# The gate projection of an SSD mixer, with tokens instead of channels on the partitions

## The chip, the cores and the metric

The kernel runs on one core of a Trainium2 chip. The metric is the time of one execution on the device, in microseconds (us). The kernel before was timed in three runs: 1871.24 us median, from 1871.17 to 1872.91.

## The reference

A two-layer diffusion backbone over 256 latent tokens and 256 context tokens, 1024 wide. Layer 0 mixes tokens with a gated DeltaNet, layer 1 with a Mamba-2 state space mixer (SSD); each layer ends in a mixture of 16 experts. The change lies in the second mixer, of which only the latent output is needed, since it is the last layer:

```python
def ssd_mixer(hx, hc, w_in, conv_w, conv_b, a_log, dt_bias, d_skip, norm_g, w_out):
    ...
    def project(h):
        p = h @ w_in
        z = p[..., :SSD_INNER]
        xbc = jax.nn.silu(depthwise_conv(p[..., SSD_INNER:SSD_INNER + SSD_CONV_CH], conv_w) + conv_b)
        ...
    def mix(h, h0f, h0b):
        z, xs, bm, cm, dt = project(h)
        yf, hf = ssd_scan(xs, dt[:, :, 0], A[0], bm, cm, h0f)
        yb, hb = ssd_scan(_rev(xs), _rev(dt[:, :, 1]), A[1], _rev(bm), _rev(cm), h0b)
        y = yf + _rev(yb) + d_skip.astype(F32).reshape(SSD_GROUPS, r)[..., None] * xs.astype(F32)
        y = y.reshape(b, t, SSD_INNER).astype(h.dtype) * jax.nn.silu(z)
        return rms_norm(y, norm_g) @ w_out, hf, hb
```

`z` is the gate: 2048 channels, projected from the 1024 inputs. `y`, the scan's result, is multiplied by silu(z), scaled by the root mean square over all 2048 channels of a token, and goes through the output projection `w_out`. Everything is in float32.

## The kernel before

A float32 matmul is made of three matmuls of split operands: a tile is copied to the type fp32r (the high half, `H`), and the remainder is the low half (`L`); the products H·H, L·H and H·L are added up. `split` (L512 on) makes the halves of a weight tile: ACT copies (L520), POOL subtracts (L522), or DVE for items whose number is in the table `DV`. The inputs lie ready in halves as `hT`, with channels on the partitions, in eight tiles of 128 channels and 512 tokens (256 of them latent).

The second mixer is a pipeline of items (`pipeline`, L534). Each item is one block of output channels of the input projection: its weights come from the queue of SP into a tile `wst` of 1 MB (two items share one), are split one item ahead, and `proj` issues 24 matmuls. Its later steps (`post`) follow, one each, behind the splits of the following items, and between items `tick` moves the waiting generators on. After the items for B and C come 16 x items (512 tokens each, `xitem`) and 16 z items (256 tokens each, `zitem`), in the order of the table `SSD_ORDER`: two of x and two of z by turns, z four pairs behind, so that the last eight z items come alone. When two x items are done, `ssd_group` is spawned: the scan for one head group of four heads in six steps. In them, `ga` (DVE) and `gw` (ACT, DVE, POOL) are weighted inputs and decay matrices, `hm` in `gb` is the state between the chunks (two POOL products, L1837, then a DVE sum, L1838), `yi` and `ya` are PE's products between and within chunks, POOL adds twice (L1855), DVE adds `ya` (L1862), PE transposes the sum, and ACT copies it to `y` (L1868) with channels on the partitions.

A z item's first step takes silu of the projection (ACT) and multiplies `y` by it (DVE, L1742). The second takes the square (ACT) and adds it to `sqs` on POOL (L1748), and makes the halves yH (ACT, L1751) and yL (DVE, L1752), scaled by the norm's gain, which is a value per partition there. The sums over channels are matmuls with ones, in `ssd_out`. At z item 13 the first tile of `w_out` is split (`ssd_wsplit`, wH on ACT, wL on DVE, L1881) and `ahead` spawned, which makes the expert layer's gate block (`moe_block`, gb, L1252) and the rows of the residual gate (`gate_rows`, g1). Then `ssd_out` runs the output projection into `acc`; after it comes the routing, and the expert layer, whose weights are loaded ahead (`moe_stream(1, 19)`) into the pool of 21 tiles of 1 MB, as they become free.

Each engine works its queue in the order in which the code issues; an instruction that waits holds up all that stand behind it on its engine.

## Time and profile before

| | us |
|---|---|
| median of three runs | 1871.24 |
| the profiled execution | 1866.32 |
| its span, first to last instruction | 1864.4 |
| PE busy in the span | 1579.6 |
| DVE busy | 833.0 |
| ACT busy | 453.7 |
| POOL busy | 405.6 |

The profiled execution lies 4.9 us below the median; sums made from its rows are set against its own time. PE's share of 85% is a mean over stages with different limits: in the expert layers the weights' loading sets the pace, in the mixers work on PE and its neighbours does. The second mixer's x and z items run from about 1176 to 1340 us, the output projection from there to 1391 us.

### The profile page before, as it was taken

How to read it: one execution, taken by the hardware profiler on the slowest of the kernel's cores; microseconds unless marked ns; L12 is line 12 of the kernel's file. 1: busy time of each engine (PE TensorE's matmuls, PEld its weight loads, DVE VectorE, ACT ScalarE, POOL GpSimd, SP SyncE). 2: the span in 40 equal slices, each digit the busy share in tenths (PEclk: the TensorE clock that was granted, in tenths of full speed). 3: DMA queues.
4: the chain of work that ended last, by engine and by line, in shares of the span. 5: the costliest groups of instructions: out<-in, count | busy, mean ns of one | idle time of the engine just before them, and what ended most of it. 6: DMA issues, size and time to landing. Idle time of an engine off the chain costs nothing.

```text
span 1864.4 us, 28211 instructions
## 1 busy us (share of the span) xinstructions
PE 1579.6 (85%) x11666; PEld 969.7 (52%) x11666; DVE 833.0 (45%) x1678; ACT 453.7 (24%) x825; POOL 405.6 (22%) x378
## 2 busy tenths in 40 slices
PE   7999888996899999989887999999899766666665
PEld 5666567864645443322226877878776332222222
DVE  4446987778632232212127877777753120111113
ACT  4552233223211100000005554666521000000001
POOL 3242255755000000000003444566400000000001
PEclk9999898998998999999998999999999887677788
DMA  9947522101888999999996441122698999999996
GB/s 305 377 161 273 181 68 91 48 1 69 310 326 355 378 383 420 419 420 420 419 409 211 158 136 46 46 69 91 236 372 351 418 419 419 419 419 420 419 419 257
DMA packets 136597, 520.18 MB, mean 279 GB/s; under 512 B 12237, under 2 KB 72022, under 8 KB 88598
## 3 DMA queue, kind: packets, MB, share of 16 engines
q1 hardware_dynamic: 136070, 517.58, 71.3%
q8 instruction: 92, 1.51, 0.3%
q0 software_dynamic: 400, 0.81, 0.1%
q14 instruction: 35, 0.29, 0.0%
HBM read 515.21 MB, written 3.15 MB: 278 GB/s over the span
## 4 chain that ended last, share of the span: by engine, by line
PE 40%; DMA 33%; DVE 16%; issue 5%; ACT 3%; POOL 2%; SPq 1%; POOLq 0%; ACTq 0%; DVEq 0%
PE ps L153 19%; DMA ew<-in_moe_w_down_dram 11%; DMA ew<-in_moe_w_up_dram 11%; PE proj L153 10%; DMA ew<-in_moe_w_gate_dram 10%; PE acc L153 3%; PE ps L157 2%; DVE adacc L384 2%; DVE tmpa L792 2%; DVE tmpb L791 2%; DMA adaq<-in_ada_w_dram 1%; PE pp L153 1%; POOL wr L522 1%; PE vn L153 1%; PE qs L153 1%
## 5 line engine op out<-in xcount | busy, mean ns | idle before, releaser
L153 PE MATMUL ps<-ew,xs 128*32 128x256 f32 (+1 forms) x3072 | 408.5, 522 | 113.9 <-DMA ew<-in_moe_w_gate_dram 58.9
L153 PE MATMUL proj<-hH,wr 128*128 128x512 f32 (+2 forms) x1312 | 380.5, 369 | 6.6 <-POOL wr L522 4.6
L153 PEld LDWEIGHTS ps<-ew,xs 128*32 128x32 f32 (+1 forms) x3072 | 136.5, 132 | 365.7 <-issue 149.7
L153 PEld LDWEIGHTS proj<-hH,wr 128*128 128x128 f32 (+1 forms) x1312 | 236.7, 190 | 57.5 <-issue 8.7
L153 PE MATMUL ps<-ew,moeblk 128*32 128x256 f32 (+3 forms) x1824 | 201.9, 455 | 47.0 <-DMA ew<-in_moe_w_down_dram 44.9
L522 POOL TENSOR_TENSOR wr<-wst,wr 128x1024 fp32r<-128x1024 f32 x74 | 184.4, 2496 | 247.4 <-ACT wr L520 247.2
L153 PE MATMUL proj<-hL,wr 128*128 128x512 f32 (+2 forms) x656 | 237.5, 362 | 0.4 <-DVE hL L2104 0.4
L1504 DVE TENSOR_TENSOR hid<-ps,sg 128x512 f32<-128x512 f32 (+1 forms) x32 | 17.9, 558 | 463.0 <-issue 271.5
L1481 DVE SCALAR_TENSOR_TENSOR ys<-ps,moeblk 32x256 f32<-32x256 f32 (+2 forms) x114 | 69.2, 607 | 225.9 <-PE ps L153 224.7
L153 PEld LDWEIGHTS ps<-ew,moeblk 128*32 128x32 f32 (+1 forms) x1824 | 75.4, 129 | 167.9 <-issue 86.4
L153 PEld LDWEIGHTS proj<-hL,wr 128*128 128x128 f32 (+1 forms) x656 | 125.1, 191 | 19.5 <-issue 1.0
L1503 ACT ACTIVATE sg<-ps 128x512 f32<-128x512 f32 (+1 forms) x32 | 15.7, 491 | 464.3 <-PE ps L153 464.3
L518 POOL CAST wr<-wdt 128x512 fp32r<-128x512 f32 x1 | 0.9, 869 | 529.4 <-PE ps L153 529.4
L2126 POOL DMA_DIRECT2D fgr<-in_final_norm_g_dram x1 | 0.6, 590 | 459.1 <-DMA ew<-in_moe_w_down_dram 459.1
L520 ACT ACTIVATE wr<-wst 128x1024 fp32r<-128x1024 f32 x79 | 82.9, 1053 | 20.3 <-POOL wr L522 9.7
L981 POOL TENSOR_SCALAR S<-S,gdnblk 128x128 f32<-128x128 f32 x128 | 74.7, 605 | 36.5 <-DVE S L990 36.4
L153 PE MATMUL ps<-G,X 128*128 128x128 f32 (+1 forms) x480 | 65.1, 298 | 9.5 <-DVE G L1362 9.5
L170 ACT ACTIVATE moeblk<-ps 128x512 f32<-128x512 f32 (+1 forms) x16 | 7.8, 491 | 265.3 <-PE ps L157 265.3
L153 PEld LDWEIGHTS ps<-G,X 128*128 128x128 f32 x480 | 62.8, 210 | 11.1 <-DVE G L1362 9.6
L560 DVE SCALAR_TENSOR_TENSOR u<-proj,prm,u 128x510 f32<-128x510 f32 (+1 forms) x56 | 39.5, 705 | 43.7 <-ACT u L558 43.6
L1382 ACT ACTIVATE xs<-ps,adaT 128x128 f32<-128x128 f32 (+1 forms) x60 | 21.3, 435 | 132.2 <-PE ps L153 120.6
L558 ACT ACTIVATE u<-proj,prm 128x512 f32<-128x512 f32 (+1 forms) x56 | 36.4, 651 | 51.0 <-PE proj L153 51.0
(417 smaller groups left out, 2189.7 us busy)
## 6 DMA issues: line engine op xcount, KB each, us to landing
ew<-in_moe_w_gate_dram SPq DMA_DIRECT2D x128, 1024.0 KB, 19.9
ew<-in_moe_w_up_dram SPq DMA_DIRECT2D x128, 1024.0 KB, 19.9
ew<-in_moe_w_down_dram SPq DMA_DIRECT2D x118, 1024.0 KB, 19.9
adaw<-in_ada_w_dram SPq DMA_DIRECT2D x40, 1024.0 KB, 9.0
wst<-in_ssd_w_in_dram SPq DMA_DIRECT2D x24, 1024.0 KB, 5.4
wst<-in_gdn_w_in_dram SPq DMA_DIRECT2D x16, 1024.0 KB, 10.9
adaq<-in_ada_w_dram SPq DMA_DIRECT2D x8, 1024.0 KB, 11.8
ew<-in_moe_w_down_dram SPq DMA_DIRECT2D x32, 256.0 KB, 6.7
```

What stands on the lines that cost most here:

```text
L153: self.nc.tensor.matmul(out, lhsT, rhs, start=start, stop=stop)
L157: self.nc.tensor.transpose(out, in_, self.ident[:k, :k])
L384: nc.vector.scalar_tensor_tensor(a, w[:, kk], c, a, op0=OP.mult, op1=OP.add)
L520: self.nc.scalar.activation(wr[:, 0, :, :m], src, AF.Copy)
L522: (self.nc.vector if dve else self.nc.gpsimd).tensor_tensor(wr[:, 1, :, :m], src, wr[:, 0, :, :m].bitcast(FT), op=OP.subtract)
L558: nc.scalar.activation(u[:, :n], p[:, :n], AF.Copy, scale=taps[1])
L560: nc.vector.scalar_tensor_tensor(v(u, 1, T), v(p, 0, T - 1), taps[0], v(u, 1, T), op0=OP.mult, op1=OP.add)
L791: nc.vector.tensor_tensor(t, bc(Lp[:, rows, j], n), mid(X[:, j, cols], m), op=OP.mult)
L792: nc.vector.tensor_tensor(X[:, rows, cols], X[:, rows, cols], t, op=OP.subtract)
L981: nc.gpsimd.tensor_scalar(S[d][1][:, h, hg, :], S[d][0][:, h, hg, :], self.eGl[:, h, d, q:q + 1], None, op0=OP.mult)
L1382: nc.scalar.activation(o, a, AF.Identity, bias=B, scale=A)
L1481: nc.vector.scalar_tensor_tensor(cols(grp["ys"][s][o], c), blk(y[q, :FW]), tg[o, 1], blk(g2[q, :FW]), op0=OP.mult, op1=OP.mult)
```

## The change

The z projection is done the other way round. `hT` becomes the stationary operand, 128 tokens at a time, and 512 columns of weights move, so that the result has tokens on the partitions. There are four blocks of 512 channels, each in two items by half of the inputs (q = 0 to 7, b = q // 2, j = q % 2), with 24 matmuls of 512 columns each, which add up in two PSUM banks `zp` that are held from the first item of a block to the end of the second. A weight tile is [512 inputs, 512 channels], and the halves lie in two tiles `wzH` and `wzL` of 128x2048. In the table, one q item follows two x items; q4 to q7 come alone at the end.

`ssd_group` ends with the sum of yt and ya, written straight into `y`, which now has tokens on the partitions; its transposes and copy are gone. The gate is done once for each block: for each 128 tokens silu (ACT), product (DVE), square with an accumulated sum over the row (ACT). One step later (`turn`), `y` is transposed to channels in two PSUM banks, and yH and yL are made from these (ACT and DVE). The sums of squares need one DVE reduction instead of the POOL sums and the matmuls with ones. The low halves of q5, q6 and q7 are made by DVE, the others by POOL. The first split of `w_out` and `ahead` are issued in the gate step of q6.

```diff
     for p in range(8 + lag):
-        o += [(k, 2 * q + j) for k, q in ((1, p), (0, p - lag)) if 0 <= q < 8 for j in range(2)]
+        o += [(1, 2 * p + j) for j in range(2) if p < 8] + [(0, p - lag)] * (p >= lag)
...
-SOW = 10
+SOW = 5
...
-ZT = 2
+ZT = 4
...
-DV = (9,11,13,15)
+DV = (5, 6, 7)
...
     def wload(self, n):
...
+            if isinstance(c, tuple):
+                b, j = c
+                t = self.u([128, KD // 2, 512], "wst")
+                src = ws["w"][j * 512:(j + 1) * 512, b * 512:(b + 1) * 512]
...
     def split(self, it, dve=None, hi=None):
 
         src = it["src"]()
+        if "acc" in it:
+            wr = [self.u([128, KD // 2, 512], f"wz{n}", FR) for n in "HL"]
+            self.nc.scalar.activation(wr[0], src, AF.Copy)
+            (self.nc.vector if it["dve"] else self.nc.gpsimd).tensor_tensor(wr[1], src, wr[0].bitcast(FT), op=OP.subtract)
+            it["wr"] = wr
+            return
...
+    def proj_tok(self, it, hT):
+
+        acc, j, wr = it["acc"], it["j"], it["wr"]
+        if j == 0:
+            acc += [self.ps("zp") for _ in range(2)]
+        it["p"] = acc
+        for k in range(4):
+            for t in range(2):
+                for a, b in ((0, 0), (0, 1), (1, 0)):
+                    self.mm(acc[t], hT[b][4 * j + k][:, t * 128:(t + 1) * 128], wr[a][:, k, :],
+                            start=j + k + a + b == 0, stop=j == 1 and k == 3 and a == 1)
...
                 if ct == 0:
-                    st["y"] = [self.u([128, 8, 256], f"y{j}") for j in range(2)]
+                    st["y"] = [self.u([128, 2, 1024], f"y{j}") for j in range(2)]
...
-        def zitem(ct):
-            def act(it):
...
-                z = self.cu([128, 256], "z")
-                y = st["y"][ct // 8][:, ct % 8]
-                nc.scalar.activation(z, it["p"][:, :256], AF.Silu)
-                nc.vector.tensor_tensor(y, y, z, op=OP.mult)
-
-            def fin(it):
-                y = st["y"][ct // 8][:, ct % 8]
-                sq = st["sq"]
-                nc.scalar.activation(sq[:, 1], y, AF.Square)
-                nc.gpsimd.tensor_tensor(sq[:, 0], sq[:, 0], sq[:, 1], op=OP.add)
-                H, L = st["yH"][ct // 8][:, ct % 8], st["yL"][ct // 8][:, ct % 8]
-                g = self.sng[:, ct:ct + 1]
-                nc.scalar.activation(H, y, AF.Copy, scale=g)
-                nc.vector.scalar_tensor_tensor(L, y, g, H.bitcast(FT), op0=OP.mult, op1=OP.subtract)
...
+        def zitem(q):
+            b, j = divmod(q, 2)
+            h = b // 2
+
+            def gate(it):
...
+                if q == SOW:
+                    st["sow"] = [self.ssd_wout(n) for n in range(3)]
+                if q == 6:
+                    st["ws"] = [self.ssd_wsplit(st, 0)]
+                    self.spawn(ahead(), 1)
+                if j == 0:
+                    return
...
+                for t in range(2):
+                    z, y = self.cu([128, 512], "z"), st["y"][h][:, t, b % 2 * 512:b % 2 * 512 + 512]
+                    nc.scalar.activation(z, it["p"][t], AF.Silu)
+                    nc.vector.tensor_tensor(y, y, z, op=OP.mult)
+                    nc.scalar.activation(z, y, AF.Square, accum_out=st["sq"][:, t, b:b + 1])
+
+            def turn(it):
+                it["yp"] = [self.ps() for _ in range(2)]
+                for n in range(4):
+                    for t in range(2):
+                        c = b % 2 * 512 + n * 128
+                        self.tr(it["yp"][n // 2][:, n % 2 * 256 + t * 128:n % 2 * 256 + t * 128 + 128], st["y"][h][:, t, c:c + 128])
+                for n in range(4):
+                    ct = 4 * b + n
+                    y, g = it["yp"][n // 2][:, n % 2 * 256:n % 2 * 256 + 256], self.sng[:, ct:ct + 1]
+                    H, L = st["yH"][h][:, ct % 8], st["yL"][h][:, ct % 8]
+                    nc.scalar.activation(H, y, AF.Copy, scale=g)
+                    nc.vector.scalar_tensor_tensor(L, y, g, H.bitcast(FT), op0=OP.mult, op1=OP.subtract)
+            return dict(src=lambda: self.wtile((b, j)), acc=zacc[b], j=j, post=[gate] + [turn] * j, dve=q in DV,
+                        ticks=ZT if q >= 8 - LAG else XT * 2)
...
-        nc.vector.tensor_tensor(fl(yt), fl(yt), intra, op=OP.add)
-        yield
-        p = self.ps()
-        for j in range(2):
-            for c in range(2):
-                self.tr(p[:, j * 256 + c * 128:j * 256 + c * 128 + 128], yt[:, c, j * 128:(j + 1) * 128])
-        nc.scalar.activation(fl(st["y"][g // 4][:, g % 4 * 2:g % 4 * 2 + 2, :]), p, AF.Copy)
+        o = st["y"][g // 4][:, :, g % 4 * 256:g % 4 * 256 + 256]
+        nc.vector.tensor_tensor(o, yt, intra.rearrange("p (c n) -> p c n", c=2), op=OP.add)
...
-                p = self.ps()
-                for t in range(2):
-                    self.mm(p[:, t:t + 1], st["sq"][:, 0, t * 128:(t + 1) * 128], self.ones[:, 0:1])
-                self.rsqrt(r2[:, 0:2], p[:, 0:2], 1.0 / 2048, EPS)
+                nc.vector.tensor_reduce(r2[:, 0:2], st["sq"], axis=AX.X, op=OP.add)
+                self.rsqrt(r2[:, 0:2], r2[:, 0:2], 1.0 / 2048, EPS)
```

POOL's queue about the scan of the seventh head group, the second last, before:

```order
L522 TENSOR_TENSOR wr<-wst,wr 128x1024
L1748 TENSOR_TENSOR sqs<-sqs 128x256
L1806 TENSOR_TENSOR gw<-gw,Gs 128x512
L1837 TENSOR_TENSOR gb<-gb,ssdblk 128x256 x2
L1840 TENSOR_TENSOR gb<-xt,gw 128x256 x2
L522 TENSOR_TENSOR wr<-wst,wr 128x1024
L1855 TENSOR_TENSOR gb<-gb,ga 128x512 x2
```

The same place after:

```order
L1892 TENSOR_TENSOR gb<-gb,ga 128x512 x2
L535 TENSOR_TENSOR wr<-wst,wr 128x1024
L525 TENSOR_TENSOR wzL<-wst,wzH 128x2048 x2
L1843 TENSOR_TENSOR gw<-gw,Gs 128x512
L1874 TENSOR_TENSOR gb<-gb,ssdblk 128x256 x2
L1877 TENSOR_TENSOR gb<-xt,gw 128x256 x2
L1892 TENSOR_TENSOR gb<-gb,ga 128x512 x2
```

`wr` and `wzL` are low halves of weights, `sqs` the sums of squares. Between two groups' additions to gb (L1855, L1892) the sums and the small splits are gone, and two splits of 128x2048, for q3 and q4, stand together ahead of this group's gw and gb. The second of them is written into the tile in which q3's high half lay.

DVE's queue ahead of the copy of the ada rows to `gb` (L1252 before, L1279 after), before:

```order
L1742 TENSOR_TENSOR y_7468<-y_7468,z 128x256
L1752 SCALAR_TENSOR_TENSOR yL<-y_7468,prm_239,yH 128x256
L522 TENSOR_TENSOR wr<-wst,wr 128x1024
L1881 TENSOR_TENSOR wL<-sow,wH 128x2048
L1742 TENSOR_TENSOR y_7468<-y_7468,z 128x256
L1752 SCALAR_TENSOR_TENSOR yL<-y_7468,prm_239,yH 128x256
L1252 COPY gb<-adaT_151 128x256
```

After, with the copy in the seventh row:

```order
L525 TENSOR_TENSOR wzL<-wst,wzH 128x2048
L1772 TENSOR_TENSOR y_7468<-y_7468,z 128x512 x2
L1888 TENSOR_TENSOR ga<-yi,ssdblk 128x512 x2
L1900 TENSOR_TENSOR y_7468<-gb,ya 128x2x256
L1913 TENSOR_TENSOR wL<-sow,wH 128x2048
L1786 SCALAR_TENSOR_TENSOR yL<-ps,prm_239,yH 128x256 x4
L1279 COPY gb<-adaT_151 128x256
L172 COPY g_9128<-ps 128x512
L1772 TENSOR_TENSOR y_7468<-y_7468,z 128x512 x2
L1786 SCALAR_TENSOR_TENSOR yL<-ps,prm_239,yH 128x256 x4
```

Products and low halves of y came by turns, item by item; now two products and four low halves stand together, with a split for q7 ahead of the products of block 2, and the split of w_out (L1913) ahead of its four low halves.

ACT's queue at the end of the mixer, before, from the copies of `moe_block` and `gate_rows` on:

```order
L1258 ACTIVATE moeblk<-ps 128x256
L170 ACTIVATE g_9384<-ps 128x512
L1741 ACTIVATE z<-proj 128x256
L1747 ACTIVATE sqs<-y_7468 128x256
L1751 ACTIVATE yH<-y_7468,prm_239 128x256
L1741 ACTIVATE z<-proj 128x256
L1747 ACTIVATE sqs<-y_7468 128x256
```

After, from the first split of w_out on:

```order
L1912 ACTIVATE wH<-sow 128x2048
L1785 ACTIVATE yH<-ps,prm_239 128x256 x4
L1285 ACTIVATE moeblk<-ps 128x256
L170 ACTIVATE g_9128<-ps 128x512
L1771 ACTIVATE z<-zp 128x512
L1773 ACTIVATE z,sq<-y_7468 128x512
L1771 ACTIVATE z<-zp 128x512
L1773 ACTIVATE z,sq<-y_7468 128x512
L1785 ACTIVATE yH<-ps,prm_239 128x256 x4
L1912 ACTIVATE wH<-sow 128x2048 x7
```

The last block's silu, for all its 512 channels, stands behind the copy of g1 (L170), and squares and silus now stand by turns, with DVE's product between them.

## Rows read from the trace of the kernel before

**Rows 1.** Windows: length; busy PE, PEld, DVE, ACT, POOL (instructions); clock; DMA share; GB/s

```profile
1211.10:1243.90 32.80, 31.15 (x185) 26.28 (x183) 21.81 (x39) 20.09 (x35) 24.35 (x20) 1.00 0.21 65
1243.90:1269.76 25.86, 25.82 (x152) 22.31 (x152) 17.98 (x35) 15.62 (x29) 17.81 (x14) 1.00 0.27 82
1299.84:1320.00 20.16, 17.23 (x118) 15.18 (x118) 14.42 (x30) 11.88 (x24) 12.10 (x11) 1.00 0.54 194
1320.00:1340.25 20.25, 16.38 (x146) 15.80 (x144) 14.50 (x15) 10.32 (x19) 8.76 (x8) 0.92 0.39 124
1390.80:1409.00 18.20, 13.80 (x109) 10.95 (x113) 12.12 (x49) 2.78 (x9) 0.00 (x0) 0.81 0.73 293
1440.00:1840.00 400.00, 267.79 (x2744) 109.82 (x2745) 49.55 (x107) 11.94 (x32) 0.59 (x1) 0.78 1.01 417
```

**Rows 2.** Timeline of SP's queue around 1400 us: start, length, what it issued

```profile
1390.98 0.89 SPq L1225 DMA_DIRECT2D ew<-in_moe_w_down_dram  x2
1408.96 2.92 SPq L1228 DMA_DIRECT2D ew<-in_moe_w_gate_dram  x4
```

**Rows 3.** Timeline of PE at the mixer's end; in brackets idle time, releaser

```profile
1311.31 1.56 PE L153 MATMUL yi<-gb,CT 128*128 128x256 f32 x6 [0.85 <-DVE gb L1838]
...
1319.37 0.66 PE L157 MATMUL ps<-ident,gb 128*128 128x128 f32 x4 [1.85 <-DVE gb L1862]
...
1332.78 2.36 PE L153 MATMUL ps<-ident,gb 128*32 128x64 f32 x32 [3.17 <-DVE gb L1252]
```

**Rows 4.** The chain that ended last: start, length, engine, tile, line, instructions

```profile
1258.38 0.86 PE ps L153 x4
...
1262.11 1.73 PE yi L153 x8
1263.84 1.73 PE ya L153 x16
1265.57 0.45 PE ps L157 x4
1266.02 2.87 PE proj L153 x24
...
1269.76 5.48 PE proj L153 x24
```

**Rows 5.** Groups by line and shape, 1140 to 1400 us: busy us, mean ns; idle

```profile
L1855 POOL TENSOR_TENSOR gb<-gb,ga 128x512 f32<-128x512 f32 x16 | 20.9, 1308 | 20.4 <-DVE ga L1851 19.8
...
L1881 DVE TENSOR_TENSOR wL<-sow,wH 128x2048 fp32r<-128x2048 f32 x8 | 18.7, 2358 | 11.6 <-ACT wH L1880 11.6
...
L1748 POOL TENSOR_TENSOR sqs<-sqs 128x256 f32<-128x256 f32 x16 | 15.7, 978 | 14.7 <-ACT sqs L1747 14.7
...
L1880 ACT ACTIVATE wH<-sow 128x2048 fp32r<-128x2048 f32 x8 | 15.0, 1907 | 15.0 <-PE acc L153 15.0
...
L1752 DVE SCALAR_TENSOR_TENSOR yL<-y,prm,yH 128x256 fp32r<-128x256 f32 x16 | 13.4, 837 | 1.2 <-ACT yH L1751 1.2
...
L1806 POOL TENSOR_TENSOR gw<-gw,Gs 128x512 f32<-128x512 f32 x8 | 10.5, 1315 | 7.5 <-ACT gw L1804 7.5
...
L1837 POOL TENSOR_TENSOR gb<-gb,ssdblk 128x256 f32<-128x256 f32 x16 | 9.5, 615 | 0.0
...
L1751 ACT ACTIVATE yH<-y,prm 128x256 fp32r<-128x256 f32 x16 | 8.1, 508 | 0.0
...
L1838 DVE TENSOR_TENSOR gb<-gb,ps 128x512 f32<-128x512 f32 x8 | 5.5, 688 | 27.3 <-POOL gb L1837 27.3
```

**Rows 6.** The same view, POOL, the first 1000 us: a subtract of 128x2048

```profile
L1120 POOL TENSOR_TENSOR wL<-gwo,wH 128x2048 fp32r<-128x2048 f32 x4 | 18.0, 4520 | 9.4 <-ACT wH L1119 9.4
```

**Rows 7.** Timeline of DVE in the period of the second window

```profile
1260.39 0.69 DVE L1838 TENSOR_TENSOR gb<-gb,ps 128x512 f32<-128x512 f32 x1 [3.02 <-POOL gb L1837]
...
1268.12 2.00 DVE L1742 TENSOR_TENSOR y<-y,z 128x256 f32<-128x256 f32 x1
```

**Rows 8.** Timeline of POOL in the same period

```profile
1267.43 2.39 POOL L522 TENSOR_TENSOR wr<-wst,wr 128x1024 fp32r<-128x1024 f32 x1
```

36 lines of the change are left out of this document (17 added, 19 removed).

## The prediction

> **What bounds the kernel now.** I began with the windows view by stage [rows 1]. From 1440.00 to 1840.00 us the expert layer moves 417 GB/s at a DMA share of 1.01: that part waits for bytes alone. In the stretch before it, 1390.80 to 1409.00, the share is only 0.73, and the list of DMA issues says why [rows 2]: SP issues the last two expert loads at 1390.98 and the next four at 1408.96. The 21 one-megabyte tiles of the pool are full by then, and loading goes on when the first experts have been used. So the prefetch already waits for the mixer, and the end of the program moves one for one with the end of the second mixer. What ends the mixer is read from the same windows: in a period in the middle (1243.90 to 1269.76) PE is busy 25.82 of 25.86 us; in the last two stretches 17.23 of 20.16 and 16.38 of 20.25. In the middle PE's own work sets the pace; at the end it idles 2.93 + 3.87 = 6.80 us. The timeline of PE there names the releaser of the longest waits [rows 3]: a DVE result, gb of the scan twice and gb of the ada block, the last for 3.17 us. The tail is a chain through POOL, DVE and ACT with matmuls in its gaps.
>
> **The change part by part.**
>
> *Matmuls.* Sixteen items of 24 matmuls with 256 columns at 2.87 us become eight of 24 with 512 columns; an x item of that shape takes 5.48 [rows 4]: 16 x 2.87 - 8 x 5.48 = 45.9 - 43.8 = 2.1 us less. Transposes: 32 of the scan's result go, 32 of the gated y come, no difference. The Trainium skill (TensorE: Matmul & The Clock Gate, section "Wait — 56ns, not 53.3ns?") gives a fixed cost of about 2.5 ns a matmul on top of the columns. By it, 192 fewer matmuls would save an estimated 0.5 us instead of 2.1; the rows here show more, and I keep the rows.
>
> *Work taken off.* POOL loses 16 adds of 978 ns, 15.7 us [rows 5], and ACT eight copies; DVE's y products become half as many and twice as wide. In the middle none of these engines bounds anything (POOL 17.81 of 25.86), so I count nothing there. At the end the freed time is inside the waits below. The weight loads stay 1 MB each and are hidden at a DMA share of 0.21 to 0.54 [rows 1]; the longer runs per row cost nothing. The tensor_reduce for the ones-matmuls is a small operation off the path.
>
> *What the order does.* Two or more z items used to stand between the scan's steps; now only one q item of 5.48 us stands in a period, and q4 to q7 close the mixer with one scan step or so between. I followed PE through the changed program, engine queues beside it, with the durations of the rows. The waits that end on PE:
>
> (a) POOL before q4. The low half of q4's weights (128x2048) lies in the slot of q3's high half, so POOL's subtract cannot start before q3's matmuls end. Behind it in POOL's queue stand gw and gb of the seventh head group, which DVE's hm add and PE's second yi matmuls need. A 128x2048 subtract on POOL took 4.52 us [rows 6], gw 1.32, two gb 1.23, the DVE add 0.69 [rows 5]: 7.8 us after q3, covered by 1.3 us of matmuls (0.86 of ps and a quarter of yi's 1.73 [rows 4]). Before, the same add waited 3.02 us for POOL [rows 7], but a z item of 2.87 us covered it. **6.4 us.** Low bound 3, if the wide subtract runs at DVE's 2.36 us; high bound 8, if DVE holds it up.
>
> (b) After that, y's product for block 1 stands on DVE behind the y sum (as 0.69), which waits for one more yi result on DVE (0.69) and two POOL adds (2 x 1.31), and behind q5's low half (2.36); then product, square, second Silu and second product in turn (0.5 to 0.7 each, by DVE's 128x512 add at 0.69 and ACT's H step, 0.51 at half that width). From q3's end y is ready at 7.8 + 1.3 + 0.7 + 2.6 + 0.7 + 2.4 + 2.5 = 18.0; PE is at its transposes at 7.8 + 1.3 + 1.73 + 0.45 + 5.48 = 16.8, after the rest of yi, ya, the transposes of u, and q4 [rows 4]: **1.2 us** (0 to 3).
>
> (c) The turn to channels makes ACT's H and DVE's L alternate, since two pairs share a PSUM bank: 4 x (0.51 + 0.84) = 5.4 us at the means of before [rows 5], and all of it ahead of the copy that feeds ga of the last group (four DVE products, later two more). One q item covers the first part: **3.1 us** over both ga steps (1 to 4).
>
> (d) The products of block 2 wait on DVE behind q7's low half (2.36), of which a yi and ya step covers little, as PE comes to the transposes right after them: **1.9 us** (0 to 3).
>
> (e) The ada block's gb copy stands on DVE behind the first w_out split (2.36) and four L steps. Before, it stood behind one split and two L steps and PE waited 3.17 us [rows 3]; now **4.9 us** (3 to 6).
>
> (f) The last block's Silu stands on ACT behind g1's copy, whose matmuls PE does after q7. Then copy, Silu, product, square, Silu, product in series, 0.5 to 0.7 each as in (b): **4.0 us** (2 to 5) with nothing but 0.9 us of transposes for PE. Before, the last item needed only its own two halves, and PE was in w_out at once.
>
> (g) The second w_out split (1.91 on ACT, 2.36 on DVE) waits for the last turn: **1.8 us** (0 to 3).
>
> (h) In the step of x12, ACT's square waits for DVE's product, which shares time with POOL's wide split; the Silu of x11 and then the copy for ga come late: **3.8 us** (0 to 6). Rows of before show what such a meeting is like: POOL's subtract from 1267.43 for 2.39 us, DVE's product from 1268.12 for 2.00 [rows 7, 8], so both end within 0.3 us of each other, whereas DVE's 128x512 add, twice as wide, takes 0.69 on average. The Trainium skill (SBUF — State Buffer, section "Who interferes with whom") calls the port pair an exclusive lock, which the first takes for its whole instruction. This trace agrees.
>
> (i) In the periods of q1 and q2 the hm add is reached with no z item ahead of yi: **2.4 us** for both (0 to 3).
>
> Sum of the waits 6.4 + 1.2 + 3.1 + 1.9 + 4.9 + 4.0 + 1.8 + 3.8 + 2.4 = 29.5 us. They take the place of PE's idle time of before: 6.80 at the end and 32.80 - 31.15 = 1.65 in the period at 1211.10 [rows 1], 8.5 in all. With the matmuls: 29.5 - 8.5 - 2.1 = **+18.9 us**. All low bounds together give 3 + 0 + 1 + 0 + 3 + 2 + 0 + 0 + 0 = 9, hence 9 - 8.5 - 2.1 = -1.6; all high ones 41 - 10.6 = +30.
>
> The profiled run of before took 1866.32 us with a span of 1864.4, the median of the three runs is 1871.24. The sum against the profiled run is 1885.2; the same 18.9 us on the median give 1890.1, the forecast.
>
> **The rivals.**
>
> *PE bound and waits hidden* (chance 0.17). The matmuls' 2.1 us remain as a gain, and half the idle time of the end goes because POOL and ACT have less to do: 1871.2 - 2.1 - 3.4 = 1865.7. For it: PE has no idle time in the middle period, and POOL loses 15.7 us. Against it: the subtract of q4 has no other place in its queue, and cover is gone where PE already waits.
>
> *Only the slot and the end count* (0.20): (a), (e) and (f) alone, 6.4 + 4.9 + 4.0 - 6.8 - 2.1 = +6.4, so 1877.6. The other waits are small and hang on the order of a microsecond; they could be absorbed by one another.
>
> *Shared port and clock* (0.07). Each of four wide POOL subtracts holds a DVE operation for 4.5 instead of 2.4 us, about 2 us on the path each: +8, 1898. The granted clock was 0.92 in the stretch with the 3.17 us wait and 1.00 in the one ahead of it [rows 1]; three waits of this size or more would add a little of the same kind.
>
> *The end does not follow the mixer* (0.06). If the expert loads could run further ahead, the loss would be hidden: 1871. Against it is the pause of 18 us in [rows 2].
>
> **How the numbers follow.** Forecast 0.50, the others 0.17, 0.20, 0.07, 0.06. The range leaves out the first rival and the upper end of the third: 1869 to 1899. About 0.2% (3.7 us) is what a measurement of this kernel can tell from no change. Faster 0.17, same 0.06, slower 0.50 + 0.20 + 0.07 = 0.77. The likeliest case's own range is 1882 to 1898.
>
> **What would show it.** Items of 24 zp matmuls at 5.48 us, eight of them; PE idle 5 to 8 us before a yi step with POOL's or DVE's gb as the releaser, right after q3; a wait of over 4 us for the ada gb; another of about 4 us before the last y transposes, with DVE's y as the releaser; the first w_out matmul some 19 us later; the pause in expert loads 15 to 20 us longer; the stretch of 400 us behind it unchanged. The forecast is wrong if PE's timeline shows fewer than 20 us of idle time between the first q item and w_out, or if the expert loads' pause stays at 18 us.

## The result and the profile after

The changed kernel takes 1882.26 us (median, 1879.4 to 1886.0) against 1871.2 us (1869.02 to 1872.91) for the kernel before: a ratio of 1.0061, with a 95% interval of 1.0040 to 1.0082. It is slower, as forecast, by 11.1 us instead of 18.9. Of the profiled executions, the changed one took 1879.40 us with a span of 1877.6, 13.1 us more than before.

I measure both traces by one stretch, used for every run below. It begins at a wait that both have, the first of two of PE's waits of 0.78 us for DVE's ga ahead of a ps group, and ends at the first w_out matmul (tile acc). Windows of before: from, to; length; busy PE, PEld, DVE, ACT, POOL (instructions); clock; DMA share; GB/s. The first is the stretch, the second goes on to the pause of the expert loads.

```profile
1164.51:1340.25 175.74, 166.14 (x1031) 142.88 (x1031) 125.58 (x235) 105.40 (x192) 107.08 (x85) 0.99 0.28 91
1340.25:1390.98 50.73, 49.09 (x234) 40.42 (x232) 27.57 (x46) 20.32 (x24) 1.48 (x2) 1.00 0.92 372
```

The same view of after. First the stretch; then the place behind q3, the end of the mixer, w_out up to the pause of the expert loads, the pause, and 400 us of the expert layer.

```profile
1161.15:1352.04 190.89, 168.40 (x839) 135.63 (x839) 106.93 (x225) 100.97 (x170) 86.36 (x63) 0.96 0.30 100
1281.98:1301.00 19.02, 12.66 (x59) 10.55 (x59) 5.78 (x11) 10.02 (x13) 10.02 (x8) 0.82 0.17 56
1340.87:1352.04 11.17, 7.60 (x57) 7.08 (x57) 2.08 (x3) 3.87 (x9) 0.00 (x0) 0.65 0.55 233
1352.04:1403.80 51.76, 50.63 (x230) 41.66 (x228) 27.82 (x48) 19.71 (x23) 0.00 (x0) 0.95 0.80 304
1403.80:1421.78 17.98, 14.29 (x109) 11.18 (x113) 11.94 (x49) 2.75 (x9) 0.00 (x0) 0.81 0.73 293
1453.00:1853.00 400.00, 274.32 (x2744) 111.65 (x2744) 48.80 (x106) 11.79 (x31) 0.59 (x1) 0.75 1.01 417
```

The stretch grew from 175.74 to 190.89 us, by 15.15. PE idles 190.89 - 168.40 = 22.49 us in it, 9.60 before (+12.89), and is busy 2.26 us longer although it has 192 instructions fewer: its clock fell from 0.99 to 0.96. Behind the stretch little changes: the pause is 17.98 us as in [rows 2], the expert layer moves the same 417 GB/s as in [rows 1], and from the first w_out matmul to the last instruction it is 524.2 us before, 525.6 after, and 523.8 to 525.5 in every run below. So the end of the program does follow the end of the mixer.

That the stretch grew by more than the profiled time did (13.1) is due to its start: this execution entered it 3.36 us earlier. All profiles of this case enter it between 1160.07 and 1170.78 us, though the code ahead of it is the same. It goes with TensorE's clock in the first expert layer: from 500 to 584 us it was 0.96 here and in the three other runs that entered ahead of 1163 us, 0.90 in before, 0.88 in the run that entered last; that the clock is the cause is not shown. Set against the kernel before, medians and stretches differ by 0.6 to 5.7 us, 2.4 on average. The waits that an edit leaves alone, however, come out alike from run to run: the last two of after, 2.00 and 1.57, are within 0.01 us of that in e1_slot, e2_dve4, e5_cover and e8_two. So the stretch, though it is one execution of each kernel, is what I read the experiments by, and the totals where they differ by more.

Timeline of PE after, the rows with a wait of over 0.4 us from 1230 us on, and the first w_out matmul: start, length, line, operation and tile; in brackets the idle time ahead and its releaser. The rows answer to [rows 3].

```profile
1233.46 1.56 PE L153 MATMUL yi<-gb,CT 128*128 128x256 f32 x6 [1.34 <-DVE gb L1875]
...
1243.44 0.98 PE L157 MATMUL ps<-ident,y 128*128 128x128 f32 x7 [0.66 <-DVE y L1772]
...
1263.28 1.56 PE L153 MATMUL yi<-gb,CT 128*128 128x256 f32 x6 [1.32 <-DVE gb L1875]
...
1295.12 2.93 PE L153 MATMUL yi<-gb,CT 128*128 128x256 f32 x6 [6.36 <-DVE gb L1875]
...
1307.10 0.98 PE L157 MATMUL ps<-ident,y 128*128 128x128 f32 x7 [0.92 <-DVE y L1772]
...
1315.95 2.14 PE L153 MATMUL ps<-ga,bt 128*128 128x256 f32 x8 [0.44 <-DVE ga L1854]
...
1330.80 0.99 PE L157 MATMUL ps<-ident,y 128*128 128x128 f32 x7 [1.46 <-DVE y L1772]
...
1340.87 2.33 PE L153 MATMUL ps<-ident,gb 128*32 128x64 f32 x32 [3.63 <-DVE gb L1279]
...
1348.76 0.30 PE L157 MATMUL ps<-ident,y 128*128 128x128 f32 x1 [2.00 <-DVE y L1772]
1350.63 1.76 PE L157 MATMUL ps<-ident,y 128*128 128x128 f32 x7 [1.57 <-DVE y L1772]
1352.04 0.78 PE L153 MATMUL acc<-wH,yH 128*128 128x512 f32 x1
```

The largest wait is the forecast one, 6.36 us right after q3, with DVE's gb as the releaser. The timelines of POOL and then of DVE show what stands behind it:

```profile
1287.47 4.50 POOL L525 TENSOR_TENSOR wzL<-wst,wzH 128x2048 fp32r<-128x2048 f32 x1 [12.20 <-PE zp L153]
1291.94 1.26 POOL L1843 TENSOR_TENSOR gw<-gw,Gs 128x512 f32<-128x512 f32 x1
1293.17 1.17 POOL L1874 TENSOR_TENSOR gb<-gb,ssdblk 128x256 f32<-128x256 f32 x2
```

```profile
1294.38 0.69 DVE L1875 TENSOR_TENSOR gb<-gb,ps 128x512 f32<-128x512 f32 x1 [7.65 <-POOL gb L1874]
```

POOL stood still for 12.20 us and was released by q3's last zp matmul. Its subtract for q4 then took 4.50 us, gw and gb came behind it, and DVE's hm add, behind those, ended at 1295.07; PE went on at 1295.12.

### The profile page after: what moved, and what is told of

Read it like the earlier page. It is cut to its first block, busy times and chain, and to the rows that moved or that the text cites. A ratio compares the mean times of both kernels' runs of the same rounds, so it can differ in the third digit from the quotient of the medians.

```text
span 1877.6 us, 27735 instructions
## 1 busy us (share of the span) xinstructions
PE 1588.8 (85%) x11470; PEld 965.1 (51%) x11470; DVE 814.5 (43%) x1670; ACT 448.3 (24%) x801; POOL 382.8 (20%) x354
## 4 chain that ended last, share of the span: by engine, by line
PE 38%; DMA 36%; DVE 16%; issue 4%; ACT 4%; POOL 2%; SPq 0%; ACTq 0%; POOLq 0%; DVEq 0%
PE ps L153 16%; DMA ew<-in_moe_w_down_dram 13%; DMA ew<-in_moe_w_up_dram 12%; DMA ew<-in_moe_w_gate_dram 10%; PE proj L153 9%; PE acc L153 3%; PE ps L157 2%; DVE adacc L384 2%; DVE tmpa L819 2%; DVE tmpb L818 2%; DMA adaq<-in_ada_w_dram 1%; PE pp L153 1%; PE vn L153 1%; PE qs L153 1%; PE ds L153 1%
## 5 line engine op out<-in xcount | busy, mean ns | idle before, releaser
L153 PE MATMUL ps<-ew,xs 128*32 128x256 f32 (+1 forms) x3072 | 412.7, 529 | 109.9 <-DMA ew<-in_moe_w_up_dram 57.8
L153 PE MATMUL proj<-hH,wr 128*128 128x512 f32 (+2 forms) x1056 | 330.9, 389 | 5.6 <-POOL wr L535 3.7
L153 PEld LDWEIGHTS proj<-hH,wr 128*128 128x128 f32 (+1 forms) x1056 | 196.7, 191 | 55.9 <-issue 9.3
L153 PE MATMUL proj<-hL,wr 128*128 128x512 f32 (+2 forms) x528 | 202.1, 383 | 0.2 <-DVE hL L2134 0.2
L535 POOL TENSOR_TENSOR wr<-wst,wr 128x1024 fp32r<-128x1024 f32 x62 | 154.5, 2499 | 232.3 <-ACT wr L533 232.1
L153 PEld LDWEIGHTS proj<-hL,wr 128*128 128x128 f32 (+1 forms) x528 | 100.8, 191 | 19.2 <-issue 1.0
L531 POOL CAST wr<-wdt 128x512 fp32r<-128x512 f32 x1 | 0.6, 611 | 524.2 <-PE ps L153 524.2
L170 ACT ACTIVATE moeblk<-ps 128x512 f32<-128x512 f32 (+1 forms) x16 | 7.8, 490 | 265.3 <-PE ps L157 265.3
L533 ACT ACTIVATE wr<-wst 128x1024 fp32r<-128x1024 f32 x63 | 66.0, 1052 | 12.5 <-PE ps L153 7.2
L587 DVE SCALAR_TENSOR_TENSOR u<-proj,prm,u 128x510 f32<-128x510 f32 (+1 forms) x56 | 39.5, 705 | 52.1 <-ACT u L585 52.0
## 6 DMA issues: line engine op xcount, KB each, us to landing
adaq<-in_ada_w_dram SPq DMA_DIRECT2D x8, 1024.0 KB, 11.9
```

The costliest lines, as they stand in the source:

```text
L153: self.nc.tensor.matmul(out, lhsT, rhs, start=start, stop=stop)
L533: self.nc.scalar.activation(wr[:, 0, :, :m], src, AF.Copy)
L535: (self.nc.vector if dve else self.nc.gpsimd).tensor_tensor(wr[:, 1, :, :m], src, wr[:, 0, :, :m].bitcast(FT), op=OP.subtract)
L587: nc.vector.scalar_tensor_tensor(v(u, 1, T), v(p, 0, T - 1), taps[0], v(u, 1, T), op0=OP.mult, op1=OP.add)
```

## The experiments

Each kernel is the changed one with the edit shown, unless something else is said. The table has the stretch of each, PE's busy and idle time and clock in it, and the ratio of the median to that of the kernel before, run beside it.

| kernel | stretch, us | busy | idle | clock | ratio (95%) |
|---|---|---|---|---|---|
| before | 175.74 | 166.14 | 9.60 | 0.99 | 1 |
| after | 190.89 | 168.40 | 22.49 | 0.96 | 1.0061 (1.0040 to 1.0082) |
| e1_slot | 186.23 | 169.77 | 16.46 | 0.96 | 1.0069 (1.0045 to 1.0092) |
| e2_dve4 | 185.57 | 168.91 | 16.66 | 0.96 | 1.0075 (1.0053 to 1.0098) |
| e3_ahead | 189.45 | 166.95 | 22.50 | 0.97 | 1.0072 (1.0046 to 1.0097) |
| e4_squares | 183.98 | 166.25 | 17.73 | 0.97 | 1.0059 (1.0041 to 1.0077) |
| e5_cover | 184.86 | 168.46 | 16.40 | 0.96 | 1.0057 (1.0042 to 1.0073) |
| e6_joint | 174.32 | 164.50 | 9.82 | 0.98 | 1.0004 (0.9989 to 1.0019) |
| e7_warm | 187.64 | 173.03 | 14.61 | 0.99 | 1.0096 (1.0076 to 1.0116) |
| e8_two | 188.79 | 158.66 | 30.13 | 0.94 | 1.0064 (1.0039 to 1.0090) |
| e9_joint_gb | 169.36 | 163.25 | 6.11 | 0.99 | 0.9974 (0.9960 to 0.9988) |
| e10_before_gb | 172.56 | 166.16 | 6.40 | 0.99 | 0.9976 (0.9963 to 0.9990) |
| e11_copy_first | 168.23 | 161.66 | 6.57 | 1.00 | 0.9968 (0.9950 to 0.9985) |
| e12_ahead_first | 169.46 | 162.24 | 7.22 | 1.00 | 0.9968 (0.9952 to 0.9984) |

The totals of the first five don't show the 1.4 to 6.9 us that their stretches lost; they lie within each other's intervals and that of after. What one edit did is read from its trace alone. Set against the kernel before, each stretch agrees with the interval of its total (that of e2_dve4 at its very edge), but for e7_warm.

**The slot of q4's weights.** A z item's split asks for one tile of the weight stream ahead instead of two, so that the low half of q4 doesn't wait for q3's slot.

```diff
-        self.wload(ws["cols"].index(key) + 2)
+        self.wload(ws["cols"].index(key) + (1 if isinstance(c, tuple) else 2))
```

> The changed kernel with one edit: weight tiles of the z items are loaded one tile ahead instead of two, so that a tile of the pool is free and the low half of q4's weights no longer lies where q3's high half was; POOL's subtract may start when x15's matmuls end, one item (5.5 us) earlier. Theory (the reuse of the slot holds POOL, and gw, gb, the hm add and yi behind it): the idle time of 6.36 us ahead of yi after q3 falls below 1.5 us, and the half clock after it goes; the whole kernel is 6 to 8 us faster than the changed kernel's 1882.3, about 1875. Rival (POOL's 4.5 us subtract and its place in the queue are the cause, whatever the slot): the wait stays over 4 us. Second rival (loading is the cover that is lost): a new wait of PE for weights at q5 to q7, 1882 or more.

The wait became 3.67 us, neither under 1.5 nor over 4: the slot is 2.7 of the 6.4 us. Timeline of PE, then of POOL:

```profile
1298.87 1.85 PE L153 MATMUL yi<-gb,CT 128*128 128x256 f32 x6 [3.67 <-DVE gb L1875]
```

```profile
1291.15 4.58 POOL L525 TENSOR_TENSOR wzL<-wst,wzH 128x2048 fp32r<-128x2048 f32 x1 [9.47 <-ACT wzH L524]
1295.68 1.27 POOL L1843 TENSOR_TENSOR gw<-gw,Gs 128x512 f32<-128x512 f32 x1
```

POOL no longer waits for PE, but for ACT: the high half of q4 (1289.08 to 1291.02) stands on ACT behind the scan's gw operations. The subtract is still the wide instruction in front of gw and gb. The waits (b) disappeared too, and that for the ada gb fell to 1.99.

**Who makes the subtract.** DVE makes q4's low half; the slot stays as it was.

```diff
-DV = (5, 6, 7)
+DV = (4, 5, 6, 7)
```

> The changed kernel with q4's low half made by DVE instead of POOL; the slot, and so the wait for q3's matmuls, stays, now on DVE. Theory (the slot holds whoever makes it): the wait ahead of yi remains, but shorter by the difference of the two subtracts and by POOL's gw and gb running beside it: 2.3 (subtract) + 1.5 (two conv steps behind it) + 0.7 (hm add) - 1.3 of cover = 3.2 us instead of 6.36; 1879. Rival (POOL's length alone): the wait goes altogether, below 1 us, 1875.

The wait became 4.02 us. Who makes the subtract counts as well as the slot. It is 0.8 more than expected for a reason that two timelines show, of DVE and of POOL:

```profile
1294.76 2.29 DVE L525 TENSOR_TENSOR wzL<-wst,wzH 128x2048 fp32r<-128x2048 f32 x1 [4.23 <-PE zp L153]
```

```profile
1295.18 3.01 POOL L1843 TENSOR_TENSOR gw<-gw,Gs 128x512 f32<-128x512 f32 x1 [12.60 <-ACT gw L1841]
```

POOL's gw, 1.29 us on average in after, took 3.01 and ended 1.1 us behind DVE's subtract, so nearly all of its usual time lies behind that. DVE's hm add then waited 0.86 us for POOL's gb. The Trainium skill (SBUF — State Buffer, section "Who interferes with whom") calls the port of the two engines an exclusive lock; this row agrees.

**The ada block earlier.** `ahead` is started in q5's gate instead of q6's.

```diff
+                if q == 5:
+                    self.spawn(ahead(), 2)
                 if q == 6:
                     st["ws"] = [self.ssd_wsplit(st, 0)]
-                    self.spawn(ahead(), 1)
```

> The changed kernel with the expert layer's gate block and the rows of g1 begun one z item earlier (in the gate step of q5 instead of q6) and in a lane of their own, so that their matmuls and copies lie between q6 and q7 and not behind q7. Theory (DVE's gb copy behind the w_out split and four low halves, and the last Silu behind g1's copy, hold PE at the end): the wait of 3.63 us for gb falls under 1 us, and the 3.57 us ahead of the last transposes become about 2.5 to 4, since less stands between; 3 to 5 us faster than 1882.3, about 1878. Rival (the chain product, low halves, w_out split sets the end in any order): the waits move to the last transposes and w_out, and the time stays within 1.5 us of 1882.

The rival was right about the size (1.4 us of the stretch), but not about the place. The wait did not move to the last transposes or w_out: it came 8.55 us earlier in the stretch and grew from 3.63 to 4.77, and the last two (2.00 and 1.64) stayed:

```profile
1333.75 2.33 PE L153 MATMUL ps<-ident,gb 128*32 128x64 f32 x32 [4.77 <-DVE gb L1279]
```

**The squares.** Both products first, both squares behind them.

```diff
+                zs = []
...
                     nc.vector.tensor_tensor(y, y, z, op=OP.mult)
-                    nc.scalar.activation(z, y, AF.Square, accum_out=st["sq"][:, t, b:b + 1])
+                    zs.append((z, y))
+                for t, (z, y) in enumerate(zs):
+                    nc.scalar.activation(z, y, AF.Square, accum_out=st["sq"][:, t, b:b + 1])
```

> The changed kernel with the two squares of a gate step behind both products instead of the first square between the first product and the second Silu, so that ACT does not wait for DVE between the two halves. Theory: product, square with its accumulator, Silu and product in turn (0.6 + 0.72 + 0.49 + 0.70 us) lose the square and the alternation, about 1.2 us at each of the transposes of blocks 1, 2 and 3: waits of 0.92, 1.46 and 3.57 us become about 0, 0.4 and 2.2; 3 to 4 us faster, 1879. Rival (the products wait for the splits in front of them, not for ACT): under 1 us.

The waits for y of 0.66, 0.92 and 1.46 us went, with the first of two for u, and the last one fell from 1.57 to 0.21: in the gate step of after the second Silu stood on ACT behind the first square, and the second product behind that Silu. ACT's timeline of after:

```profile
1241.46 0.63 ACT L1773 ACTIVATE z<-y 128x512 f32<-128x512 f32 x1 [7.90 <-DVE y L1772]
...
1242.09 0.58 ACT L1771 ACTIVATE z<-zp 128x512 f32<-128x512 f32 x1
```

The waits that went are 4.8 us of idle time, and 2.2 of busy time came with it, at a clock of 0.97; hence 6.9, more than the 3 to 4 expected.

**The cover of the scan's steps.** Items q0 to q3 take half as many steps of the scan between them.

```diff
-                        ticks=ZT if q >= 8 - LAG else XT * 2)
+                        ticks=ZT if q >= 8 - LAG else XT)
```

> The changed kernel with half as many scan steps after each of q0 to q3 (two instead of four), so that yi stands behind the next x item (q4 for the seventh head group) and not straight behind the ga matmuls. The stretch compared is from PE's wait of 0.78 us for ga (at 1161.15 in the changed kernel) to the first w_out matmul: 175.7 us before, 190.9 changed, 186.2 with the slot freed, 184.0 with the squares behind. Theory (lost cover): the waits of 1.34 and 1.32 us for the hm add vanish; of the 6.36 us after q3 the subtract of 4.5 us less 1.3 us of matmuls stays, 3.2 us, now with POOL's low half of q4 as the releaser; stretch 190.9 - 2.6 - 3.2 - 1.4 (half clock) = about 184, and 6 to 7 us off the total. Rival (the steps only wait elsewhere, at the y transposes, which come later in the period): stretch 188 or more.

The waits of 1.34 and 1.32 us for the hm adds are gone, and so are that of 0.85 for ACT's gw behind q0 and the three in the step of x12 (0.66, 0.39, 0.26); of the 6.36 remains 2.80: PE now comes to q4's low half ahead of that yi, and waits there for the subtract itself. The wait for the last group's ga grew from 0.44 to 2.44 us:

```profile
1291.28 0.80 PE L153 MATMUL zp<-wzL,hH 128*128 128x512 f32 x1 [2.80 <-POOL wzL L525]
...
1313.68 2.93 PE L153 MATMUL ps<-ga,bt 128*128 128x256 f32 x8 [2.44 <-DVE ga L1854]
```

**The three together.** The diffs of the slot, the squares and the cover, as above.

> The changed kernel with three edits together: half the scan steps after q0 to q3, weight tiles loaded one ahead (slot free), and the squares behind both products. Theory: what is left is the matmuls' 2.1 us gain, the wait for the ada gb (2 to 3.6 us), and the last block's chain (about 2.2 us): stretch from the ga wait to w_out about 175 to 178 us against 175.7 before, total within 3 us of before (ratio 0.999 to 1.003). Rival (the token layout costs by itself, in the wide splits and the turn to channels): stretch over 181, ratio over 1.004.

The stretch is 174.32 us, 1.4 below the kernel before, and the total can't be told from it (1.0004, 0.9989 to 1.0019). So the changed layout's loss lies in these waits. Three edits were made at once, and what each gave alone is in its run above. What is left is at the end:

```profile
1303.08 2.14 PE L153 MATMUL ps<-ga,bt 128*128 128x256 f32 x8 [2.47 <-DVE ga L1857]
...
1326.62 2.33 PE L153 MATMUL ps<-ident,gb 128*32 128x64 f32 x32 [3.61 <-DVE gb L1279]
...
1334.65 0.30 PE L157 MATMUL ps<-ident,y 128*128 128x128 f32 x1 [1.99 <-DVE y L1773]
```

**The clock by itself.** 72 matmuls of zeros are put into the changed kernel where PE waits: 40 ahead of the yi behind q3, 16 ahead of the ada gb, 16 ahead of the last transposes. The waits for the other engines stay.

```diff
+        if g == 6:
+            self.warm(40)
         inter = [self.ps("yi") for _ in range(2)]
...
             def turn(it):
+                if q == 7:
+                    self.warm(16)
...
+            self.warm(16)
             self.moe_block(1, 1)
```

> The changed kernel with dummy matmuls (zeros, 256 columns) on PE inside its waits: 40 ahead of the yi after q3, 16 ahead of the ada gb, 16 ahead of the last y transposes. Nothing else moves; they end before the waits do. Theory (PE falls to the lower clock in waits of 2 us and more, and this costs after them): yi's six matmuls 1.56 instead of 2.93 us, the first w_out matmuls at 0.23 us from start to start instead of 0.43; stretch 2 to 4 us shorter than 190.9. Rival (the dummy matmuls only stand in the way, or the clock's loss is absorbed by the next wait): within 1 us of 190.9.

The stretch fell by 3.25 us and its clock rose to 0.99. The yi group behind q3 still took 2.90 us; 2.01 us of idle time were left behind the 40 matmuls and the two yi matmuls that follow them. But w_out's first matmuls came 0.23 us apart and not 0.43. With that a wait appears that the slow matmuls had hidden, for the second w_out split:

```profile
1303.77 2.90 PE L153 MATMUL yi<-gb,CT 128*128 128x256 f32 x6 [2.01 <-DVE gb L1878]
...
1364.38 0.50 PE L153 MATMUL acc<-wL,yH 128*128 128x512 f32 x1 [1.01 <-DVE wL L1918]
```

The total doesn't show the gain: its median is 17.6 us above the kernel before, the stretch 11.9. In the profiled run the stretch was entered at 1169.79, 8.64 us later than in after, which accounts for its longer time (5.08 us); why the median of the four runs is as high stays open. What the zeros gained is thus shown by one trace and by no total.

**Less work for PE.** The third product of the z projection (low weights by high activations) is left out: 64 of 192 matmuls, 64 x 0.228 = 14.6 us.

```diff
-                for a, b in ((0, 0), (0, 1), (1, 0)):
+                for a, b in ((0, 0), (0, 1)):
...
-                            start=j + k + a + b == 0, stop=j == 1 and k == 3 and a == 1)
+                            start=j + k + a + b == 0, stop=j == 1 and k == 3 and b == 1)
```

> The changed kernel with the third product (low half of the weights) of the z projection left out, 64 of 192 matmuls, 64 x 0.228 = 14.6 us of PE's work; the halves are still made. Theory (order and queues set a good part of the mixer): the waits take up a part, and the stretch from the ga wait to w_out shrinks by 5 to 10 us, with longer waits for gb, y and splits. Rival (PE's work sets the mixer): by 13 to 15 us.

The stretch lost 2.1 us, less than either theory said. PE's busy time fell by 9.7 instead of 14.6, as the clock went down to 0.94, and its idle time rose by 7.6:

```profile
1337.93 2.33 PE L153 MATMUL ps<-ident,gb 128*32 128x64 f32 x32 [5.41 <-DVE gb L1279]
```

The q items are the cover of the waits. Shorter, they leave longer waits behind them (5.41 for the ada gb, 3.13 and 3.14 for the hm adds of q1 and q2; only the one behind q3 got shorter, 5.46), and the yi groups behind the hm adds take 2.93 us instead of 1.56.

**The ada gb out of the end.** The joint kernel with the ada block's gb copy made on DVE in q5's gate, ahead of the w_out split; and, as its counterpart, the kernel before with the same copy made in the step of z11. In both, moe_block then takes that copy instead of making its own.

```diff
+                if q == 5:
+                    self.gbpre = self.gbcopy(1, 1)
                 if q == SOW:
```

> The joint kernel (half the scan steps after q0 to q3, slot free, squares behind the products) with one more edit: DVE's copy of the ada rows to gb is made in the gate step of q5, ahead of the last w_out split and low halves. Theory: the wait of 3.61 us for gb ahead of the 32 ada matmuls goes; g1's copy, Silu and products follow as much earlier, as far as DVE's low halves of block 2 let them; the stretch from the ga wait to the first w_out matmul falls from 174.3 to 169 to 172 us (175.7 before), the total below before: ratio 0.996 to 0.999. Rival (the low halves of block 2 and the products behind them on DVE set the end): the wait moves in front of the last transposes, stretch 173 to 175, ratio 1.000.

```diff
+                if ct == 11:
+                    self.gbpre = self.gbcopy(1, 1)
                 if ct == SOW:
```

> The kernel before with the same edit alone, the gb copy made in the step of z11. Theory: the 3.17 us wait for gb at 1332.78 goes, and since the last two z items do not depend on it, the stretch falls from 175.7 to about 173; ratio 0.998 to 0.999. Rival: the wait moves to the last z items' splits or products, 175 or more, ratio 1.000. With the other run of this call it tells whether the token layout, with its waits taken out, beats the channel layout with the same care: theory 169 to 172 against 173.

Both did what was expected: 169.36 us in the new layout, 172.56 in the old, and both beat the kernel before (0.9974 and 0.9976). With the gb copy moved in both, the new layout's stretch is 3.2 us shorter; the totals don't tell the two apart. It isn't a comparison with equal care: the new layout has three more edits, and the waits that are left in the old one (1.84 us for the y sum ahead of the transposes, 1.20 for ga, 0.85 for the hm add) were not worked on. What is left in the first, PE's waits:

```profile
1311.61 2.88 PE L153 MATMUL ps<-ga,bt 128*128 128x256 f32 x8 [2.48 <-DVE ga L1865]
...
1338.11 0.30 PE L157 MATMUL ps<-ident,y 128*128 128x128 f32 x1 [1.99 <-DVE y L1781]
...
1346.33 0.50 PE L153 MATMUL acc<-wL,yH 128*128 128x512 f32 x1 [1.04 <-DVE wL L1924]
```

**The x item's copies ahead of the turn**, on top of that; then the ada block's rows earlier too, on a lane of their own.

```diff
-            for lag in (1, 2, 3, 4):
+            for lag in ((1, 3, 2, 4) if "acc" in items[min(i, N - 1)] else (1, 2, 3, 4)):
```

> The joint kernel with the early gb copy, and one more edit: in a step of the z items, the transposes and copies of the x item come ahead of the turn of y to channels, so that ACT's copy to xt no longer stands behind four alternations of H and L. Theory (the turn's alternation holds the last group's ga): the wait of 2.48 us for ga ahead of the last group's matmuls falls under 0.5 us; stretch 169.4 - 2.0 to 2.5 = about 167, and the lower clock after that wait goes too. Rival (ga waits for q6's low half on DVE, which stands in front as well): the wait stays over 1.5 us, stretch 169.

```diff
                 if q == 5:
+                    self.spawn(ahead(), 2)
                     self.gbpre = self.gbcopy(1, 1)
...
-                    self.spawn(ahead(), 1)
```

> The kernel of the other run of this call with the ada gate rows begun in the gate step of q5 and in a lane of their own, so that their 48 matmuls lie ahead of q7, between yi and ya, and the last Silu no longer stands behind g1's copy. Theory: the 3.3 us of ada matmuls fill waits there, the last products start 0.6 us earlier, but PE has nothing left to do while Silu and product run after q7; stretch 0 to 2 us shorter than about 167. Rival (the ada matmuls were cover for DVE's low halves of block 2 at the end; without them the last products wait for these): stretch 1 to 2 us longer.

The first cut the wait for ga from 2.48 to 1.48 and lengthened the one for u ahead of it from 0.40 to 1.55: a result just below the rival's 1.5 and far from the theory's 0.5. PE's idle time didn't fall (6.11 to 6.57 us); the 1.1 us that the stretch lost are in its busy time, at a clock of 1.00. In the second the stretch grew by 1.2, as much as the rival said if counted from the first, but at another place: the last waits stayed as they were (1.99 and 0.28), and a wait for the gb copy is new, which stands on DVE behind q7's low half. PE in the second:

```profile
1317.60 1.37 PE L153 MATMUL ps<-ident,gb 128*32 128x64 f32 x32 [0.95 <-DVE gb L1267]
```

Both are at 0.9968 of the kernel before. The kernels with the gb copy moved, in either layout, take 1862.73 to 1865.47 us, and their totals don't rank them.

## Why the prediction was right in sign and too high in size

Terms of the sum, each with what PE's timeline after shows:

| step | forecast | measured |
|---|---|---|
| (a) subtract of q4 | 6.4 | 6.36 |
| (b) y of block 1 | 1.2 | 0.92 |
| (c) turn, ga | 3.1 | 0.44 |
| (d) y of block 2 | 1.9 | 1.46 |
| (e) ada gb | 4.9 | 3.63 |
| (f) y of the last block | 4.0 | 2.00 + 1.57 = 3.57 |
| (g) second w_out split | 1.8 | 0 |
| (h) step of x12 | 3.8 | 0.66 + 0.39 + 0.26 = 1.31 |
| (i) hm add of q1, q2 | 2.4 | 1.34 + 1.32 = 2.66 |
| sum | 29.5 | 20.4 |

**What held.** The q items are 24 zp matmuls 0.228 us apart, 5.5 us as in [rows 4]. PE's own work and its waits set the end, and the end moved with them: the first w_out matmul came 11.79 us later in a profile that entered 3.36 us earlier, and from there w_out lost another 1.03 (51.76 against 50.73) at a clock of 0.95. All places with a new wait were named but for one of 0.38 us behind (b) and one of 0.85 for ACT's gw in the period of q0 (1205.03), and the releasers are those forecast. For (a) the mechanism is confirmed from both sides: without the slot 2.7 of it go, with another engine 2.3. Of the signs named, PE's idle time from the first q item (1190.33) to w_out is 22.49 us, over the 20 below which the forecast was to be wrong; the wait for the ada gb, at 3.63 us, missed its 4.

**What was mis-sized.** Three terms make 7 of the 9.1 us: (c), (g), (h). Two groups of after, by line and shape, show it for (c) and (h): operation, tiles, shapes, count; busy us and mean ns; idle time ahead and its releaser.

```profile
L1786 DVE SCALAR_TENSOR_TENSOR yL<-ps,prm,yH 128x256 fp32r<-128x256 f32 x16 | 7.3, 480 | 5.8 <-ACT yH L1785 5.8
...
L1772 DVE TENSOR_TENSOR y<-y,z 128x512 f32<-128x512 f32 x8 | 7.1, 885 | 7.1 <-ACT z L1771 7.1
```

In (c) I took the L step at the mean of before, 837 ns [rows 5]; in the turn it takes 480, and H 468. The alternation is also looser than four pairs in a row, 3.8 us: the third H runs beside the second L, and the last turn takes 3.4 us, from 1351.57 to 1355.00, instead of 5.4. So the q item covers nearly all of it.

The mean of before was one over three cases. Of its sixteen L steps four met nothing of POOL and took 0.47 us; eleven met one of POOL's adds to sqs and took 0.66 to 0.96; one met a subtract and took 2.62. Timelines of DVE and of POOL in before:

```profile
1298.88 0.47 DVE L1752 SCALAR_TENSOR_TENSOR yL<-y,prm,yH 128x256 fp32r<-128x256 f32 x1
...
1307.26 0.96 DVE L1752 SCALAR_TENSOR_TENSOR yL<-y,prm,yH 128x256 fp32r<-128x256 f32 x1
...
1324.01 2.62 DVE L1752 SCALAR_TENSOR_TENSOR yL<-y,prm,yH 128x256 fp32r<-128x256 f32 x1
```

```profile
1323.76 2.59 POOL L522 TENSOR_TENSOR wr<-wst,wr 128x1024 fp32r<-128x1024 f32 x1
```

Most of the mean's excess over 0.47 thus came from the adds to sqs, which the change itself takes away. In three of the four turns of after POOL does nothing beside the L steps. In the first, three of the four L steps lie beside a subtract of 4.62 us and the fourth begins beside its last 0.2, and they take 0.48 each all the same:

```profile
1248.61 0.48 DVE L1786 SCALAR_TENSOR_TENSOR yL<-ps,prm,yH 128x256 fp32r<-128x256 f32 x1
1249.63 0.88 DVE L1786 SCALAR_TENSOR_TENSOR yL<-ps,prm,yH 128x256 fp32r<-128x256 f32 x2 [0.55 <-ACT yH L1785]
```

```profile
1246.64 4.62 POOL L525 TENSOR_TENSOR wzL<-wst,wzH 128x2048 fp32r<-128x2048 f32 x1 [5.76 <-ACT wzH L524]
```

The tiles tell this turn from the step at 1324.01: L read y and yH before, both from SBUF, where the kernel's tiles lie; in the turn it reads yH from there and the transposes from PSUM, where PE's results lie. The Trainium skill (SBUF — State Buffer, section "Who interferes with whom") says that a DVE instruction with two SBUF inputs contends with a GpSimd instruction that reads SBUF, and that one with at most one SBUF input, outside the 2-port perf modes, does not. These rows agree, and I had not applied it to the changed operand.

In (h) I took DVE's product beside a subtract as the usual case, from [rows 7, 8]. In before it was: nine of its sixteen products took 1.96 to 2.58 us beside one. In after one of eight does (2.25 us at 1239.17), and what it meets is the 2.39 us subtract of an x item, not POOL's wide split; the seven others take 0.69, and the mean is 885 ns. (g) was right in the engines and wrong in what PE would be doing: w_out's first matmuls come 0.43 us apart and so need the split later. With the clock kept up the wait is there, 1.01 and 1.04 us.

**What was missing.** The clock was a rival's term only. Idle time grew by 12.9 us, yet the stretch by 15.15, though the matmuls became cheaper. PE's work is the same in after and in e11_copy_first: 168.40 us at a clock of 0.96, 161.66 at 1.00. So the lower clock costs 6.7 us in the stretch against full clock. At one place it can be read off directly: the yi group of six takes 1.56 us in the periods and 2.93 behind the 6.36 us wait. The matmul term holds: at full clock before's work would be an estimated 0.99 x 166.14 = 164.5 us, 2.8 more than 161.66, where the sum had 2.1; with a clock read to 0.01 the estimate is good to about 0.8. The estimated 0.5 us that follow from the fixed cost in the Trainium skill (TensorE: Matmul & The Clock Gate, section "Wait — 56ns, not 53.3ns?") differ from this, and the measurement decides.

So two errors met: 9.1 us too much waiting, and 168.40 - (166.14 - 2.1) = 4.4 us of clock left out of the sum. 18.9 - 9.1 + 4.4 is 14.2; the rest of the stretch's 15.15 is idle time outside the nine steps, such as the 0.85 and 0.38 us above. That the forecast came as near as it did is in part luck: the two errors have opposite signs.

**The pause.** "15 to 20 us longer" was wrong; it kept its 17.98 us and only moved, from 1390.98 to 1403.80 at its start and from 1408.96 to 1421.78 at its end, 12.82 both. SP's queue says why, in before and then in after:

```profile
1352.79 11.20 SPq L1228 DMA_DIRECT2D ew<-in_moe_w_up_dram  x4
1364.09 10.31 SPq L1228 DMA_DIRECT2D ew<-in_moe_w_gate_dram  x4
```

```profile
1365.66 11.20 SPq L1255 DMA_DIRECT2D ew<-in_moe_w_up_dram  x4
1376.96 10.31 SPq L1255 DMA_DIRECT2D ew<-in_moe_w_gate_dram  x4
...
1403.80 0.90 SPq L1252 DMA_DIRECT2D ew<-in_moe_w_down_dram  x2
1421.78 2.92 SPq L1255 DMA_DIRECT2D ew<-in_moe_w_gate_dram  x4
```

I had read the pause as the time from a full pool to the first experts. But the last loads ahead of it wait as well, for tiles that come free in w_out (11.20 and 10.31 us in both; of SP's waits from 1340 to 1425 us in after, 39.5 us are for acc matmuls), and move along with it. By my own last sentence a pause of 18 us should have made the forecast wrong. It didn't, because the pause isn't the measure of the prefetch: the end moved by what the mixer moved, which is what the step needed. The sentence was a bad test.

**The rivals.** That PE's work would hide the waits is excluded by the waits themselves, 22.49 us against 9.60, and by e8_two: with 14.6 us less of that work the stretch lost 2.1. "Only the slot and the end" gave 1877.6, nearer than my forecast (4.7 below the median, mine 7.8 above). But its three waits are 13.6 of the 20.4 us; the small ones it left out are there one by one, and taking some of them away (e4_squares) pays. Shared port and clock: the port holds one y product of eight, and beside POOL's five wide subtracts only two groups of ga products are longer (3.77 us at 1219.38 and 1.85 at 1274.70 instead of 1.43), with no wait of PE of 0.2 us or more in the 8 us behind either; the clock, which that rival had as a little more, is the larger part, 4.4 us. That the end doesn't follow the mixer is excluded by the 523.8 to 525.6 us from the first w_out matmul to the end in all fourteen profiles.

What stays open is why the profiles enter the stretch up to 10.7 us apart, and why the median of e7_warm is as high as it is.
